# Loading the first eight heads of v by partition halves in an attention-times-value kernel

## The chip, the cores and the metric

The kernel runs on one core of a Trainium2 chip. A core has five engines with their own instruction streams: TensorE (PE) multiplies and transposes, VectorE (DVE) and ScalarE (ACT) copy between the memories, GpSimd (POOL) and SyncE (SP) issue the DMA transfers here, and POOL also builds masks and does one cast. Sixteen DMA engines move data between HBM and the on-chip memory SBUF, which has 128 partitions; matmuls write to PSUM. Time is the device time of one execution in microseconds (us); lower is better.

## The reference

```python
batch, n_heads, seq, head_dim = 8, 12, 1024, 64
attn_weights: (8, 12, 1024, 1024) fp32;  v: (8, 12, 1024, 64) fp32

return np.einsum('bhqs,bhsd->bhqd', attn_weights, v).astype(np.float32)
```

For each of 96 heads a 1024 x 1024 matrix is multiplied by a 1024 x 64 matrix. attn_weights is 403 MB, v and the output 25 MB each.

## The kernel before

Heads are taken four at a time (`VH = 4`): 24 groups q, each split into two units, 48 units n in all. Unit n is one load of attn_weights, `load_attn(n)`: 128 partitions x 16 row groups x 1024, cast from fp32 to bf16 by the DMA itself, 4096 KB in SBUF, into one of two buffers `abf[n % 2]`. All such loads are issued by POOL on its queue; in a loop over n, POOL waits until PE has transposed unit n, then issues the load of unit n + 2. Loads 0 and 1 are issued ahead of everything, and are called loads by their unit number below; load 2 is the third.

For each unit PE transposes 16 groups (`transpose_g`, line 146 in the profile), DVE and ACT copy them to `at` (line 276), PE multiplies them with v (`multiply`, line 191), the products are copied to `ot` (line 288), transposed back (line 176) and copied to the output tile `osb` (line 259). In every first unit of a group PE first spreads the group's v: `spread_v` (line 163) reads `vr`, in which v lies as bf16 with eight heads over 128 partitions, 16 partitions to a head, 4096 elements to a partition. The spread result is copied to `vbf` (line 252). Before it, PE waits for `s_vr` to count the groups whose v is there (line 210).

v arrives in `vr` by casting DMAs on POOL's queue (`load_v`, line 352), eight or sixteen heads at a time, except the first eight heads, groups 0 and 1. These come as fp32 into two output slots of `osb` that are not used yet (`v32`), 2 MB on SP's own queue, in two transfers of 1 MB: the first half of the columns of all 128 partitions (line 136), issued before the block in which all engines work, and the second half of the columns (line 413), issued by SP inside it. The block begins for every engine when the first transfer has landed; only POOL's loads 0 and 1 are issued without that wait. DVE sets constants to zero (lines 327 to 331), and casts the first half in two instructions of 1024 columns (line 334). POOL makes the masks `ident` and `spread` (lines 372 and 383), which PE needs before its first transpose, then waits for the second transfer and for DVE's casts (`s_v0`), casts the second half (line 393, 2048 columns), and raises `s_vr` by 2. Only then does its loop begin, with the load of unit 2.

After its transfer SP raises two counters: `s_free`, which lets ACT write output slots, and `s_half`, on which PE waits in the middle of each unit and which holds PE back while a burst of stores is under way.

Of the kernel before, what the change touches and what calls it, by code (L numbers as in the profile page):

```python
# [10 lines left out]
def kernel(  # L11
# [18 lines left out]
    nc = tc.nc  # L30
# [4 lines left out]
    B, H, Q, S = attn_weights.shape  # L35
    D = v.shape[-1]
    NH = B * H
    P = 128
# [4 lines left out]
    HP = P // 2  # L43
    KW = S // (2 * P)
    SB = S // P
    V8 = 2 * VH
    VB = S // (P // V8) // SB
# [10 lines left out]
    V_SLOT = 4  # L58
    V_AT_ONCE = 4
    V_LOADS = {2: 2, **{q: V_AT_ONCE for q in range(V_AT_ONCE, NV, V_AT_ONCE)}}  # L60

    V_REST = ((0, P),)
    HALVED = NU - 2
    TOGETHER = 8
    BURSTS = {8: ((0, 8),), 16: ((8, 2), (10, 6))}
# [3 lines left out]
    def slot(q):  # L69
        return q % NO  # L70
# [12 lines left out]
    def v_n(q, fours):  # L83
        return v_h[ds(q * VH, fours * VH)].rearrange(
            "(n eight) (p r) d -> (eight p) n (r d)", eight=V8, p=P // V8
        )
# [17 lines left out]
    vr = sb("vr", [P, V_AT_ONCE // 2, VB, SB * D], bf16)  # L104
    vbf = sb("vbf", [P, SB, VH, D], bf16)
    ot = sb("ot", [P, GH, P], fp32)
    osb = sb("osb", [P, NO, 2 * G, D], fp32)

    v32 = osb[:, ds(V_SLOT, 2)].rearrange("p n r d -> p n (r d)")
    v_first = v_n(0, 2)[:, 0].rearrange("p (half x) -> p half x", half=2)  # L110
    vr_first = vr[:, 0].rearrange("p (half b) x -> p half (b x)", half=2)
    bank = [nc.alloc_psum_tensor(f"bank{i}", [P, 512], fp32).ap() for i in range(8)]
    pt = [b.rearrange("p (k j) -> p k j", k=KW) for b in bank[:4]]
    po = bank[4:6]
# [5 lines left out]
    s_v0, s_v = sem("s_v0"), sem("s_v")  # L120
# [11 lines left out]
    s_const, s_vr = sem("s_const"), sem("s_vr")  # L132

    s_half, s_free = sem("s_half"), sem("s_free")

    nc.sync.dma_start(out=v32[:, 0], in_=v_first[:, 0])

    with tc.tile_critical(sync_engine=mybir.EngineType.Pool, no_gpsimd_drain=True):
        pe = nc.tensor
# [189 lines left out]

        for h in range(2):  # L330
            nc.vector.memset(ot[:, :, ds(h * HP, HP)], 0.0).then_inc(s_ot)
        for half in range(2):
            part = ds(half * (SB * D * VB // 4), SB * D * VB // 4)
            last = nc.vector.tensor_copy(out=vr_first[:, 0, part], in_=v32[:, 0, part])  # L334
        last.then_inc(s_v0)
        engine(True)
        engine(False)
        nc.scalar.wait_ge(s_held, 16 * (BY_SYNC - HELD_FROM) // 2)
# [2 lines left out]
        pool = nc.gpsimd  # L341

        def load_attn(n):
            pieces = [(0, G)] if n < HALVED else [(0, GH), (GH, GH)]
            for g0, gn in pieces:
                pool.dma_start(  # L346
                    out=abf[n % 2][:, ds(g0, gn)].rearrange("p g s -> p (g s)"),
                    in_=attn_q[n // 2][:, ds((n % 2 * G + g0) * S, gn * S)],
                ).then_inc(s_abf[n % 2] if g0 == 0 else s_second[n], 16)

        def load_v(q, fours):
            pool.dma_start(  # L352
                out=vr[:, ds(q % V_AT_ONCE // 2, fours // 2)].rearrange("p n b x -> p n (b x)"),
                in_=v_n(q, fours),
            ).then_inc(s_v, 16)

        def store(q, fours, eng, done):
            eng.wait_ge(s_out, 2 * (q + fours) + 1)
            at_slot = osb[:, ds(slot(q), fours)].rearrange("p n r d -> p n (r d)")
            eng.dma_start(  # L360
                out=out_n(q, fours), in_=at_slot,
                **({"single_packet": True} if eng is pool and fours == 2 else {}),
            ).then_inc(done, 16)

        def store_2(q):
# [7 lines left out]
            out=ident,  # L373
            in_=ident,
# [9 lines left out]
            out=spread,  # L384
            in_=spread,
# [3 lines left out]
            pattern=[[-P, V8], [-1, P + VB - 1]],  # L389
            channel_multiplier=VB,  # L390
        ).then_inc(s_const)
        pool.wait_ge(s_v0, 16 * len(V_REST) + 1)
        pool.tensor_copy(out=vr_first[:, 1], in_=v32[:, 1]).then_inc(s_vr, 2)  # L393
        for n in range(NU - 2):
            q, i = n // 2, n % 2
            if i == 0 and q + 1 in V_LOADS:
                pool.wait_ge(s_sp, 4 * (q + 1))
                load_v(q + 1, V_LOADS[q + 1])
            pool.wait_ge(s_t[True], (n + 1) * PER_DVE)
            load_attn(n + 2)  # L400
            if i == 0 and q % TOGETHER == 0 and 0 < q <= HELD_FROM:
                for q0, fours in BURSTS[q]:
                    store(q0, fours, pool, s_osb)
# [5 lines left out]

        for p0, pn in V_REST:
            nc.sync.dma_start(
                out=v32[ds(p0, pn), 1], in_=v_first[ds(p0, pn), 1]
            ).then_inc(s_v0, 16)
        nc.sync.sem_inc(s_free, NO // 2)
        nc.sync.sem_inc(s_half, WHOLE[0])
        for k in range(1, NV // 2):
# [9 lines left out]
        for n in range(HALVED, NU):  # L428
# [8 lines left out]
            out=out_q[NV - 1], in_=osb[:, slot(NV - 1)].rearrange("p r d -> p (r d)")  # L437
# [35 lines left out]
```

## Time and profile before

| | us |
|---|---|
| median of 3 runs | 1051.83 |
| lowest and highest | 1051.76, 1052.38 |
| the profiled execution | 1051.83 |
| its span on the core | 1050.0 |

| engine | busy, us | share of the span |
|---|---|---|
| PE | 795.4 | 76% |
| DVE | 388.7 | 37% |
| ACT | 410.6 | 39% |
| POOL | 39.1 | 4% |

The span runs from the first instruction to the last. The page's slices give for each fortieth of it the busy share of each engine and of the 16 DMA engines in tenths. The timeline gives an instruction's start and duration, and in brackets how long the engine had been idle before it and what ended that; `x64` means 64 of them merged. In the timeline "SPq" and "POOLq" are the issuing of transfers, not their landing. A stretch view gives the busy time of every engine between two times, then the granted clock, the share of the DMA engines' time that packets took, and GB/s; a packet counts in the stretch in which it begins, so short stretches can have a share above 1. GB/s are bytes written: a load of attn_weights reads two bytes for each one that it writes.

### The profile page before, as it was taken

Reading aid. Unit: us, or ns where it says so; the run is one execution under the profiler, and the core shown is the slowest. Engines: PE = TensorE matmul, PEld = TensorE weight load, DVE = VectorE, ACT = ScalarE, POOL = GpSimd, SP = SyncE. Lnnn points to the kernel's source line nnn. Section 1 sums busy time; section 2 is a strip of 40 time slices with the busy share of each in tenths; the row PEclk is TensorE's granted clock in tenths of the full one; section 3 lists DMA queues with packets and bytes.
Section 4 is the critical chain, followed back from the end, with each engine's and each line's share of the span. In section 5 each row is a group of like instructions: output and inputs, shape, how many; then the busy total and the mean of one; then the engine's idle time right before and its main releaser. Section 6 shows DMA issues by size and latency. Waiting matters only on the chain.

```text
span 1050.0 us, 17183 instructions
## 1 busy us (share of the span) xinstructions
PE 795.4 (76%) x7304; PEld 708.4 (67%) x7304; DVE 388.7 (37%) x583; ACT 410.6 (39%) x493; POOL 39.1 (4%) x68
## 2 busy tenths in 40 slices
PE   0878789489789492887949779859568975887995
PEld 0777678478678482777848678647547865776885
DVE  1443344235334251343424344324223432453443
ACT  0444344335335251343425344334224433444443
POOL 1000000000000000000000000000000000000000
PEclk9989889799898796889879989889878988899898
DMA  9999999999999999999999999999999999999999
GB/s 232 229 218 219 217 216 212 217 220 218 217 218 216 212 216 379 217 218 217 207 218 220 220 218 217 207 224 212 324 275 217 218 206 220 217 220 220 209 218 352
DMA packets 12198, 240.20 MB, mean 229 GB/s; under 512 B 1056, under 2 KB 1056, under 8 KB 1056
## 3 DMA queue, kind: packets, MB, share of 16 engines
q0 software_dynamic: 11344, 233.84, 99.1%
q1 hardware_dynamic: 848, 6.29, 1.5%
q8 instruction: 3, 0.05, 0.0%
q14 instruction: 3, 0.02, 0.0%
HBM read 427.82 MB, written 25.17 MB: 431 GB/s over the span
## 4 chain that ended last, share of the span: by engine, by line
DMA 71%; PE 26%; issue 1%; POOL 0%; ACT 0%; DVE 0%; ACTq 0%; SPq 0%; POOLq 0%
DMA abf<-in_attn_weights_dram 63%; PE bank L146 22%; DMA out_dram<-osb 8%; PE bank L163 3%; PE bank L191 1%; PE bank L176 1%; POOL vr L352 0%; ACT vbf L252 0%; ACT osb L259 0%; DVE osb L259 0%; ACT ot L288 0%; POOL abf L346 0%; ACTq L259 0%; SPq L424 0%; SPq L423 0%
## 5 line engine op out<-in xcount | busy, mean ns | idle before, releaser
L146 PE MATMUL bank<-ident,abf 128*128 128x128 f32 x3072 | 430.0, 307 | 215.3 <-DMA abf<-in_attn_weights_dram 188.2
L146 PEld LDWEIGHTS bank<-ident,abf 128*128 128x128 f32 x3072 | 420.4, 212 | 227.1 <-DMA abf<-in_attn_weights_dram 195.6
L276 DVE COPY at<-bank 128x1024 bf16<-128x1024 bf16 x480 | 319.7, 689 | 405.1 <-PE bank L146 400.6
L276 ACT COPY at<-bank 128x1024 bf16<-128x1024 bf16 x288 | 287.9, 1012 | 332.0 <-PE bank L146 332.0
L191 PE MATMUL bank<-at,vbf 128*64 128x256 bf16 x3072 | 225.7, 285 | 0.0
L191 PEld LDWEIGHTS bank<-at,vbf 128*64 128x64 bf16 x3072 | 203.7, 111 | 19.4 <-issue 6.3
L288 DVE COPY ot<-bank 128x512 f32<-128x512 f32 x48 | 33.2, 692 | 208.6 <-PE bank L191 208.6
L288 ACT COPY ot<-bank 128x512 f32<-128x512 f32 x48 | 28.1, 585 | 185.9 <-PE bank L191 185.9
L163 PE MATMUL bank<-vr,spread 32*128 32x512 bf16 x768 | 87.0, 375 | 0.6 <-issue 0.2
L176 PE MATMUL bank<-ident,ot 128*128 128x128 f32 x392 | 62.4, 312 | 29.4 <-ACT vbf L252 28.7
L176 PEld LDWEIGHTS bank<-ident,ot 128*128 128x128 f32 x392 | 51.3, 159 | 41.4 <-ACT vbf L252 40.5
L259 ACT COPY osb<-bank 128x512 f32 (+1 forms) x97 | 53.4, 588 | 31.2 <-PE bank L176 29.3
L163 PEld LDWEIGHTS bank<-vr,spread 32*128 32x128 bf16 x768 | 35.2, 93 | 44.0 <-issue 1.7
L346 POOL DMA_DIRECT2D abf<-in_attn_weights_dram x50 | 26.9, 538 | 788.7 <-PE bank L146 787.7
L252 ACT CAST vbf<-bank 128x512 bf16<-128x512 f32 x48 | 25.8, 589 | 74.4 <-PE bank L163 74.4
L252 DVE CAST vbf<-bank 128x512 bf16<-128x512 f32 x48 | 30.9, 686 | 29.1 <-PE bank L163 29.1
L276 ACT ACT_TABLE_LOAD x12 | 15.4, 1283 | 6.7 <-DMA osb<-in_v_dram 6.5
L352 POOL DMA_DIRECT2D vr<-in_v_dram x6 | 4.0, 674 | 136.3 <-PE bank L163 136.3
L360 POOL DMA_DIRECT2D out_dram<-osb x5 | 3.9, 786 | 12.0 <-ACT osb L259 12.0
L393 POOL CAST vr<-osb 128x2048 bf16<-128x2048 f32 x1 | 1.9, 1889 | 22.0 <-DMA osb<-in_v_dram 22.0
L327 DVE MEMSET ident<- 128x128 f32 x1 | 0.2, 165 | 6.5 <-DMA osb<-in_v_dram 6.5
L334 DVE CAST vr<-osb 128x1024 bf16<-128x1024 f32 x2 | 2.2, 1138 | 0.0
(9 smaller groups left out, 5.3 us busy)
## 6 DMA issues: line engine op xcount, KB each, us to landing
abf<-in_attn_weights_dram POOLq DMA_DIRECT2D x46, 4096.0 KB, 29.2
vr<-in_v_dram POOLq DMA_DIRECT2D x5, 2048.0 KB, 15.3
out_dram<-osb POOLq DMA_DIRECT2D x1, 8192.0 KB, 41.7
abf<-in_attn_weights_dram POOLq DMA_DIRECT2D x4, 2048.0 KB, 23.0
out_dram<-osb POOLq DMA_DIRECT2D x3, 2048.0 KB, 33.4
out_dram<-osb POOLq DMA_DIRECT2D x1, 6144.0 KB, 41.7
osb<-in_v_dram SPq DMA_DIRECT2D x2, 1024.0 KB, 15.7
out_dram<-osb SPq DMA_DIRECT2D x1, 2048.0 KB, 14.4
```

Of the source, the lines that this page charges most:

```text
L146: last = pe.matmul(out=pt[g % 4][:, k], lhsT=words[:, k], rhs=ident, is_transpose=True, start=(k == 0), stop=(k == KW - 1),)
L163: last = pe.matmul(out=banks[h], lhsT=spread[rows, j, ds(VB - 1 - b, P)], rhs=vr[rows, n // 2, b], start=(b == 0), stop=(b == VB - 1),)
L176: last = pe.matmul(out=ps[:, ds(j * P, P)], lhsT=ot[:, j0 + j], rhs=ident, is_transpose=True, start=(j == 0), stop=(j == jn - 1),)
L191: last = pe.matmul(out=outs, lhsT=vbf[:, 2 * kw + par, h], rhs=at[:, ds(half * GH, GH), kw, ds(h * VP, VP), par], start=(n == 0), stop=(n ...
L252: copy(out=vbf[:, :, h], in_=ps.rearrange("p (k d) -> p k d", k=SB)).then_inc(s_vbf)
L259: return copy(out=rows.rearrange("p (half j) d -> p j half d", half=2)[:, ds(j0, jn)], in_=ps[:, ds(0, jn * P)].rearrange("p (j half d) -> ...
L276: ins = copy(out=at[:, g].rearrange("c k j two -> c (k j two)"), in_=bank[g % 4].bitcast(bf16),)
L288: copy(out=ot.rearrange("c j (h p) -> c h j p", h=VH)[:, ds(2 * e, 2)], in_=po[e].rearrange("c (h j p) -> c h j p", h=2, j=GH),).then_inc( ...
L334: last = nc.vector.tensor_copy(out=vr_first[:, 0, part], in_=v32[:, 0, part])
L346: pool.dma_start(out=abf[n % 2][:, ds(g0, gn)].rearrange("p g s -> p (g s)"), in_=attn_q[n // 2][:, ds((n % 2 * G + g0) * S, gn * S)],).th ...
L352: pool.dma_start(out=vr[:, ds(q % V_AT_ONCE // 2, fours // 2)].rearrange("p n b x -> p n (b x)"), in_=v_n(q, fours),).then_inc(s_v, 16)
L360: eng.dma_start(out=out_n(q, fours), in_=at_slot, **({"single_packet": True} if eng is pool and fours == 2 else {}),).then_inc(done, 16)
```

## The change

The first eight heads of v still come as 2 MB of fp32 on SP's queue, but are cut by heads and not by columns: heads 0 to 3 lie on partitions 0 to 63, heads 4 to 7 on partitions 64 to 127.

- Ahead of the block SP issues two transfers of 512 KB: partitions 0 to 63, first and second half of the columns. Inside it, one transfer of 1 MB: partitions 64 to 127, all 4096 columns.
- DVE casts partitions 0 to 63 in two instructions of 2048 columns, and raises `s_vr` by 1 itself: group 0's v is there.
- POOL does not cast ahead of its loop. In the loop's first turn, after the load of unit 2, it waits for the third transfer, casts partitions 64 to 127 in one instruction of 4096 columns, and raises `s_vr` by 1 for group 1.

```diff
-    v32 = osb[:, ds(V_SLOT, 2)].rearrange("p n r d -> p n (r d)")
-    v_first = v_n(0, 2)[:, 0].rearrange("p (half x) -> p half x", half=2)
-    vr_first = vr[:, 0].rearrange("p (half b) x -> p half (b x)", half=2)
+    v32 = osb[:, ds(V_SLOT, 2)].rearrange("p n r d -> p (n r d)")
+    v_first = v_n(0, 2)[:, 0]
+    vr_first = vr[:, 0].rearrange("p b x -> p (b x)")
+    four = [ds(0, HP), ds(HP, HP)]
+    VC = S * V8 * D // P // 2
+    part = [ds(0, VC), ds(VC, VC)]
...
-    nc.sync.dma_start(out=v32[:, 0], in_=v_first[:, 0])
+    for x in part:
+        nc.sync.dma_start(out=v32[four[0], x], in_=v_first[four[0], x])
...
-        for half in range(2):
-            part = ds(half * (SB * D * VB // 4), SB * D * VB // 4)
-            last = nc.vector.tensor_copy(out=vr_first[:, 0, part], in_=v32[:, 0, part])
-        last.then_inc(s_v0)
+        for x in part:
+            last = nc.vector.tensor_copy(out=vr_first[four[0], x], in_=v32[four[0], x])
+        last.then_inc(s_vr)
...
-        pool.wait_ge(s_v0, 16 * len(V_REST) + 1)
-        pool.tensor_copy(out=vr_first[:, 1], in_=v32[:, 1]).then_inc(s_vr, 2)
         for n in range(NU - 2):
...
             load_attn(n + 2)
+            if n == 0:
+                pool.wait_ge(s_v0, 16)
+                pool.tensor_copy(out=vr_first[four[1]], in_=v32[four[1]]).then_inc(s_vr)
...
-        for p0, pn in V_REST:
-            nc.sync.dma_start(
-                out=v32[ds(p0, pn), 1], in_=v_first[ds(p0, pn), 1]
-            ).then_inc(s_v0, 16)
+        nc.sync.dma_start(out=v32[four[1]], in_=v_first[four[1]]).then_inc(s_v0, 16)
```

More of the change, by code (lines that the diff above doesn't have):

```diff
@@ L60 @@
     V_LOADS = {2: 2, **{q: V_AT_ONCE for q in range(V_AT_ONCE, NV, V_AT_ONCE)}}
-    V_REST = ((0, P),)
     HALVED = NU - 2
```

## The prediction

> **What bounds the kernel now.** I read the page's 40 slices and queue shares first, then the chain, then the start of the timeline, then busy time by stretch.
>
> ```profile
> span 1050.0 us, 17183 instructions
> ...
> DMA  9999999999999999999999999999999999999999
> ...
> q0 software_dynamic: 11344, 233.84, 99.1%
> q1 hardware_dynamic: 848, 6.29, 1.5%
> HBM read 427.82 MB, written 25.17 MB: 431 GB/s over the span
> ...
> DMA 71%; PE 26%; issue 1%; POOL 0%; ACT 0%; DVE 0%; ACTq 0%; SPq 0%; POOLq 0%
> ...
> abf<-in_attn_weights_dram POOLq DMA_DIRECT2D x46, 4096.0 KB, 29.2
> ...
> osb<-in_v_dram SPq DMA_DIRECT2D x2, 1024.0 KB, 15.7
> ```
>
> The 16 DMA engines are busy in every slice, and the two queues' packets fill 100.6% of them: POOL's queue q0 carries the loads of attn_weights, SP's q1 the first 2 MB of v and the last stores. The chain is 71% DMA; its 26% of PE is the wait of a load that may only be issued when its buffer has been read. Whether that wait empties the queues is read from the timeline's start:
>
> ```profile
> 27.68 9.31 PE L146 MATMUL bank<-ident,abf 128*128 128x128 f32 x64 [27.68 <-DMA abf<-in_attn_weights_dram]
> 37.23 3.63 PE L163 MATMUL bank<-vr,spread 32*128 32x512 bf16 x32 [0.24 <-issue]
> 37.30 0.57 POOL L346 DMA_DIRECT2D abf<-in_attn_weights_dram  x1 [3.00 <-PE bank L146]
> 39.20 1.29 DVE L252 CAST vbf<-bank 128x512 bf16<-128x512 f32 x2 [1.48 <-PE bank L163]
> 47.76 7.95 PE L146 MATMUL bank<-ident,abf 128*128 128x128 f32 x64 [0.21 <-DMA abf<-in_attn_weights_dram]
> 56.02 0.53 POOL L346 DMA_DIRECT2D abf<-in_attn_weights_dram  x1 [18.16 <-PE bank L146]
> 67.13 3.26 PE L146 MATMUL bank<-ident,abf 128*128 128x128 f32 x14 [6.13 <-DMA abf<-in_attn_weights_dram]
> ```
>
> Load 0 lands at 27.7 us, load 1 at about 47.5, load 2 at 67.1. Load 2 is issued at 37.30, ten microseconds before load 1 has drained, and load 3 at 56.02, eleven before load 2 has. So the queue never runs dry: engine time that PE, POOL or DVE lose here is hidden as long as it stays under about ten microseconds, and time that the DMA engines lose is not hidden by anything. The stretches say the same (columns: stretch, then each engine's busy time, granted clock, DMA share, GB/s written):
>
> ```profile
> 0.00:1.50 1.50, 0.00 (x0) 0.00 (x0) 0.00 (x0) 0.00 (x0) 0.36 (x5) 1.00 0.00 0
> 47.50:67.10 19.60, 13.29 (x137) 12.69 (x136) 7.33 (x11) 8.21 (x10) 0.53 (x1) 0.95 1.00 216
> 952.10:971.40 19.30, 13.23 (x137) 12.68 (x137) 7.33 (x11) 9.48 (x11) 0.53 (x1) 0.95 1.01 217
> ```
>
> Nothing moves before 1.5 us; a load then takes 67.13 - 47.76 = 19.4 us, near the start and near the end alike. Its 4096 KB are 128 rows of 32 KB, eight for each of 16 engines, 2.42 us each, writing 216 GB/s (the source is fp32, so it reads twice that).
>
> **The change part by part.** *The first transfers.* Before, 1 MB of v over 128 partitions goes first:
>
> ```profile
> 0.74 0.38 SPq L136 DMA_DIRECT2D osb<-in_v_dram  x1
> 1.34 1.23 POOL L346 DMA_DIRECT2D abf<-in_attn_weights_dram  x2 [0.90 <-POOLq L457]
> 6.33 0.33 SPq L413 DMA_DIRECT2D osb<-in_v_dram  x1
> 6.47 0.17 DVE L327 MEMSET ident<- 128x128 f32 x1 [6.47 <-DMA osb<-in_v_dram]
> ```
> ```profile
> 1.00:2.00 1.00, 0.00 (x0) 0.00 (x0) 0.00 (x0) 0.00 (x0) 0.66 (x1) 1.00 0.39 74
> 2.00:3.00 1.00, 0.00 (x0) 0.00 (x0) 0.00 (x0) 0.00 (x0) 0.57 (x2) 1.00 0.80 229
> 3.00:4.00 1.00, 0.00 (x0) 0.00 (x0) 0.00 (x0) 0.00 (x0) 0.00 (x0) 1.00 0.85 360
> 4.25:4.50 0.25, 0.00 (x0) 0.00 (x0) 0.00 (x0) 0.00 (x0) 0.00 (x0) 1.00 0.93 393
> 4.75:5.00 0.25, 0.00 (x0) 0.00 (x0) 0.00 (x0) 0.00 (x0) 0.00 (x0) 1.00 4.87 1147
> ```
>
> The packets count in the stretch in which they start, so the jump at 4.75 is the first large packets of load 0: from 1.5 to about 4.75 us the engines carry v alone, at up to 393/0.93 = 423 GB/s, which is 3.3 GB/s into each of 128 partitions. No row shows any partition taking more. After the change the same bytes go in two transfers to 64 partitions, so at the old rate each would have to take twice as much. That is the disputed price. Lower end: the writes follow, cost 0. Upper end: packets to half the partitions take twice as long. In the page's row q1 fills 1.5% of 16 x 1050 us = 252 us with 768 data packets of 8 KB (6.29 MB; the other 80, 16 for each of its five transfers, only count up semaphores), 0.33 us each; v's 2.1 MB are 256 of them, 84 us, or 5.25 us on each of the 16 engines. Doubled, that is +5.25 us.
>
> I place it between the ends by what writes beside it, with 212 GB/s (half of 423) as the ceiling for half the partitions. While v is alone: 2 to 3 us falls from 229 to 212, 3 to 4 from 360 to 212, the last 0.75 us from about 420 to 212, and the slow first microsecond stays: 17 + 148 + 156 = 321 KB late, which is 0.76 us at 423 GB/s. Those 321 KB, 2.5 packets per engine, then alternate with load 0's packets, and the third transfer (4096 elements on 64 partitions, four packets of 16 KB per engine, 0.66 us each by doubling 0.33) alternates throughout. There the extra is at most 2.5 x 0.33 + 4 x 0.66 = 3.5 us, if the engines that write to the same partitions always do so in step, and near 0 if they are out of step, since all others then write only load 0 at 216 GB/s over 128 partitions. The start is common to all engines, which speaks for in step; the long packets between drift. I take half, 1.75 us. Sum: 0.76 + 1.75 = +2.5 us.
>
> [...] No row here shows a transfer to 64 partitions.
>
> *The wait to begin.* All engines but POOL's first two loads wait for the first transfers: DVE's memset and ACT's table load start at 6.47, ended by that DMA. With 2.5 packets per engine left at 4.75, each behind a 2.42 us packet of load 0, the first transfers land about 2.5 x (2.42 + 0.66) = 7.7 us later, near 14. Behind that stand DVE's memsets, POOL's two masks, and SP's third transfer:
>
> ```profile
> 8.01 0.28 POOL L372 TENSOR_SCALAR_AFFINE_SELECT ident<-ident 128x128 f32<-128x128 f32 x1 [5.43 <-DVE spread L328]
> 8.43 1.97 POOL L383 TENSOR_SCALAR_AFFINE_SELECT spread<-spread 128x1080 bf16<-128x1080 bf16 x1
> 32.41 1.89 POOL L393 CAST vr<-osb 128x2048 bf16<-128x2048 f32 x1 [22.00 <-DMA osb<-in_v_dram]
> ```
>
> PE may start when the masks are done, 10.40 - 6.47 = 3.9 us after the entry: near 18 us, against load 0's 27.7. Cost 0; the entry would have to be after 23.7 to make PE late and after about 33 to empty the queue. SP's releases of half units and output slots stand behind its third transfer, first needed by PE in the middle of unit 0, after 30 us: hidden too.
>
> *DVE's casts.* Two of 64 x 2048 in place of two of 128 x 1024.
>
> ```profile
> L334 DVE CAST vr<-osb x2: 629/1138/1646, 8.8 to 9.3; 128x1024 bf16<-128x1024 f32 x2
> ```
>
> By columns they double: from 2 x 1.26 to 2 x 3.3 us (the 1646 ns one ran beside POOL's mask). They end by 14 + 2.5 + 6.6 = 23 us, and PE reads them at 37.23: 0. Their increment alone now releases PE's first spreading of v.
>
> *POOL's cast* moves behind load 2. It took 1.89 us for 2048 columns; for 4096, 1.9 us if it goes by elements and 3.8 by columns; I take 3.8, from 37.9 to 41.7. Being taken from ahead of load 2 gains nothing: it ended at 34.30, and the row of 37.30 shows load 2 waiting 3.00 us more, for PE. Queued behind it on POOL is load 3, at 56.02; the third transfer, issued near 14, lands by 14 + 4 x (2.42 + 1.31) = 29 plus a few microseconds, so its wait is over. Beside it run DVE's two casts of 39.20. Lower bound of the delay 0, upper 3.8 us if POOL keeps DVE out; unit 0 then ends near 51.5, unit 1's load 3 is issued near 60, still seven before load 2's landing at 67.1. Cost 0 at either end.
>
> *The sum* against the profiled execution: 1051.83 us, which is the median of the runs itself (span 1050.0 and 1.8 around it), + 2.5 = 1054.3 us.
>
> **The rivals.** *Full halving:* all 5.25 us, in step throughout, 1057.1. For it: a common start for all engines; against it: 88% of the traffic it alternates with writes at half the rate (2.42 of 2.75 us).
>
> *The halves cost nothing:* 1051.8. An engine that reads ahead could go on reading load 0 while v's writes drain: a load writes half of what it reads, so its write side has room. For it, 216 GB/s written in stretches where 423 have been seen. Against it, the first three microseconds have no load to read. If reading ahead hides all of the alternation, +0.8 remains, 1052.6, also no change by the bound.
>
> *Faster, a tighter start:* from 1.5 to about 47.5 us the engines need 46.0 us for two loads and v, where 2 x 19.4 + 5.25 = 44.0 would do. If two shorter transfers queued back to back and a third in half as many packets recover that, -2.0 us, 1049.8. Place: the DMA shares of 0.39 to 0.85 in the first three microseconds. It decides where the first transfers' packets take less than 1.2 times as long as before. Against it: the ramp is that of the first packets, whoever issues them.
>
> *The late entry binds:* slower, if the first transfers land after 33 us; 1 us for each beyond. The 2.5 packets late would have to be more than eight; next to excluded.
>
> **How the numbers follow.** Forecast (partial halving, own range 1053.3 to 1056.0) 0.47, of which 0.05 ends within 0.2% (2.1 us, below 1053.9; about what a measurement of this kernel can tell from no change); full halving 0.25; nothing or nearly nothing 0.20; tighter start 0.07, of which 0.05 beyond the bound, since its price could be short by what the trace does not show; late entry 0.01. Slower 0.42 + 0.25 + 0.01 = 0.68, same 0.05 + 0.20 + 0.02 = 0.27, faster 0.05. The range reaches from 1051.6, just under the free case, to 1057.2, just over the full one: what it leaves out is the tighter start and the tails.
>
> **What the changed profile would show.** Right: the first v transfers land near 14 us and not 6; q1's share rises from 1.5% to 1.7 or 1.8%; PE's units 1 and 2 start near 50 and 69.6 us where they started at 47.76 and 67.13, and the end is later by that same 2.5 us, with loads still 19.4 us apart. POOL's cast stands after load 2's issue with no wait for its DMA. Wrong: unit 2 starts at 67.1 or earlier (the halves are free, or the start tighter), or the shift of unit 2 is not the shift of the end, which would put the cause somewhere else than in these 2 MB.

## The result

| | us |
|---|---|
| before, median of 9 runs (lowest, highest) | 1051.84 (1051.73, 1052.38) |
| changed, median of 9 runs (lowest, highest) | 1054.59 (1054.03, 1057.14) |
| changed, the profiled execution | 1057.1, span 1055.3 |
| ratio changed to before | 1.0031, 95% interval 1.0022 to 1.0041 |

The changed kernel is slower by about 2.75 us. It also spreads over 3.1 us where the kernel before spreads over 0.65, and the execution that was profiled is one of the slowest, 5.3 us over the profiled one of before. The queue rows of its page, to hold against those of before:

```profile
DMA  9999999999999999999999999999999999999998
...
q0 software_dynamic: 11344, 233.84, 98.7%
q1 hardware_dynamic: 800, 6.29, 1.7%
q8 instruction: 3, 0.05, 0.0%
q14 instruction: 3, 0.02, 0.0%
HBM read 427.82 MB, written 25.17 MB: 429 GB/s over the span
```

The bytes are the same, the engines are as full, and SP's queue q1 takes 1.7% of their time where it took 1.5%. The start of the timeline shows where the end came from (the columns are start, duration, instruction, and the idle time before it):

```profile
0.74 1.18 SPq L139 DMA_DIRECT2D osb<-in_v_dram  x2
19.06 0.47 SPq L415 DMA_DIRECT2D osb<-in_v_dram  x1
19.22 0.17 DVE L330 MEMSET ident<- 128x128 f32 x1 [19.22 <-DMA osb<-in_v_dram]
21.52 3.25 DVE L336 CAST vr<-osb 64x2048 bf16<-64x2048 f32 x2
29.68 9.38 PE L149 MATMUL bank<-ident,abf 128*128 128x128 f32 x64 [29.68 <-DMA abf<-in_attn_weights_dram]
39.35 0.57 POOL L348 DMA_DIRECT2D abf<-in_attn_weights_dram  x1 [15.67 <-PE bank L149]
39.97 3.59 POOL L403 CAST vr<-osb 64x4096 bf16<-64x4096 f32 x1
51.95 7.95 PE L149 MATMUL bank<-ident,abf 128*128 128x128 f32 x64 [2.33 <-DMA abf<-in_attn_weights_dram]
71.27 1.13 PE L149 MATMUL bank<-ident,abf 128*128 128x128 f32 x4 [6.09 <-DMA abf<-in_attn_weights_dram]
```

The block begins at 19.2 us and not at 6.5; that costs nothing here, since PE still starts when load 0 lands (29.68). Units 0, 1 and 2 start 2.0, 4.2 and 4.1 us later than before (27.68, 47.76, 67.13). The loads after that come as far apart as before (unit 4 starts at 114.79 where it started at 110.68, again 4.1 later), so all but the last 1.1 us of the 5.3 is lost before load 2 has landed. Most of that rest comes in two steps, between units 16 and 18 (the shift goes from 4.2 to 4.8 us) and between units 32 and 34 (4.9 to 5.3), where the two bursts of stores are issued; why is not shown. By stretch, the first microseconds (share of DMA time and GB/s are the last two columns):

```profile
1.00:2.00 1.00, 0.00 (x0) 0.00 (x0) 0.00 (x0) 0.00 (x0) 0.66 (x1) 1.00 0.00 0
2.00:3.00 1.00, 0.00 (x0) 0.00 (x0) 0.00 (x0) 0.00 (x0) 0.58 (x2) 1.00 1.02 197
4.25:4.50 0.25, 0.00 (x0) 0.00 (x0) 0.00 (x0) 0.00 (x0) 0.00 (x0) 1.00 3.85 786
```

With the engines full (a share of 1.02), v alone moves at 197 GB/s; before, it reached 393 at a share of 0.93. By the packet records, load 0's first long packet begins at 4.20 us (4.75 before), and most of the first sixteen in the half microsecond after it (the jump of the third row).

The trace also records each packet on q1. Their durations, taken from those records of the profiled executions, are what most of the experiments turn on:

| kernel | v alone, before load 0's first packet | then, beside load 0 | third transfer |
|---|---|---|---|
| before | 8 KB: 0.31 us when steady, 118 of the first transfer's 128 begun | 8 KB: 0.31 | 8 KB: 0.32 |
| changed | 8 KB: 0.59 on average, 60 of the first two transfers' 128 begun | 8 KB: 0.34 | 16 KB: 1.11 (0.62 to 1.57) |

So half of the first megabyte was left when load 0 began; it then alternated with load 0's rows of 2.43 us (the last of it begins at 15.8 us) at 0.34 us each, little more than the old 0.31, and the third transfer's rows took 1.11 us on average where 0.64 is twice the short row.

### The profile page after: what moved, and what is told of

It reads as the page before. It is cut to its first block, busy times and chain, and to the rows that moved or that the text cites. A ratio compares the mean times of both kernels' runs of the same rounds, so it can differ in the third digit from the quotient of the medians.

```text
span 1055.3 us, 17183 instructions
## 1 busy us (share of the span) xinstructions
PE 796.4 (75%) x7304; PEld 708.7 (67%) x7304; DVE 389.7 (37%) x583; ACT 410.9 (39%) x493; POOL 41.4 (4%) x68
## 4 chain that ended last, share of the span: by engine, by line
DMA 71%; PE 26%; issue 1%; POOL 0%; ACT 0%; DVE 0%; ACTq 0%; SPq 0%; POOLq 0%
DMA abf<-in_attn_weights_dram 63%; PE bank L149 22%; DMA out_dram<-osb 8%; PE bank L166 3%; PE bank L194 1%; PE bank L179 1%; POOL vr L354 0%; ACT vbf L255 0%; ACT osb L262 0%; DVE osb L262 0%; ACT ot L291 0%; POOL abf L348 0%; ACTq L262 0%; SPq L424 0%; SPq L423 0%
## 5 line engine op out<-in xcount | busy, mean ns | idle before, releaser
L279 ACT ACT_TABLE_LOAD x12 | 15.4, 1283 | 19.4 <-DMA osb<-in_v_dram 19.2
L330 DVE MEMSET ident<- 128x128 f32 x1 | 0.2, 165 | 19.2 <-DMA osb<-in_v_dram 19.2
L403 POOL CAST vr<-osb 64x4096 bf16<-64x4096 f32 x1 | 3.6, 3591 | 0.0
L336 DVE CAST vr<-osb 64x2048 bf16<-64x2048 f32 x2 | 3.2, 1662 | 0.0
```

Source lines behind the costliest of these rows:

```text
L279: ins = copy(out=at[:, g].rearrange("c k j two -> c (k j two)"), in_=bank[g % 4].bitcast(bf16),)
L403: pool.tensor_copy(out=vr_first[four[1]], in_=v32[four[1]]).then_inc(s_vr)
```

## The experiments

Two theories at the start. *Halves:* writing to 64 of the 128 partitions is what costs. *Order:* the other edits cost it, that is two transfers in place of one ahead of the block, the late start of the block, or the moved cast.

**cols_order: all of the change but the halves** (the first two transfers are now quarters of the columns, the third the other half; the casts follow the same cut, and POOL raises `s_vr` by 2 for both groups; these edits are left out below)

```diff
-        nc.sync.dma_start(out=v32[four[0], x], in_=v_first[four[0], x])
+        nc.sync.dma_start(out=v32[:, x], in_=v_first[:, x])
...
-        nc.sync.dma_start(out=v32[four[1]], in_=v_first[four[1]]).then_inc(s_v0, 16)
+        nc.sync.dma_start(out=v32[:, rest], in_=v_first[:, rest]).then_inc(s_v0, 16)
```

> Everything of the changed kernel is kept (two transfers ahead of the block, POOL's cast behind load 2) but the cut: v is again cut by columns, every transfer to 128 partitions. Theory of the halves (writes to 64 partitions are slower): the loss is gone, 1051.5 to 1052.3, the first transfers land near 6.5 us, PE's unit 2 starts near 67.1. Rival (two transfers in place of one, or the moved cast, cost the time): 1054 to 1057 as the changed kernel.

Measured: 1053.31 us median (1052.38 to 1055.31), ratio 1.0015, interval 1.0006 to 1.0024. This is neither theory's number. Its timeline shows why it is no clean comparison:

```profile
38.29 1.90 POOL L404 CAST vr<-osb 128x2048 bf16<-128x2048 f32 x1
41.19 6.29 PE L167 MATMUL bank<-vr,spread 32*128 32x512 bf16 x32 [3.77 <-POOL vr L404]
63.95 0.53 POOL L349 DMA_DIRECT2D abf<-in_attn_weights_dram  x1 [23.76 <-PE bank L150]
```

Cut by columns, group 0 needs POOL's half too, which now comes behind load 2: PE waits 3.77 us, then runs the spreading in 6.3 us where it took 3.6 (the granted clock was 0.56 from 41.2 to 47.5 us; before, it was 1.00 from 37.2 to 40.9), and load 3 is issued at 63.95, eight microseconds later than before. A moved cast needs a cut by heads; front_split below is the control that this run was meant to be. What makes up the 1.4 us of this run stays open: in its profiled execution, 0.9 us over before, all 40 slices of the page have the DMA engines busy for 90% or more.

**front_halves: only the first transfer in halves** (the rest as before)

```diff
-    nc.sync.dma_start(out=v32[:, 0], in_=v_first[:, 0])
+    for p0 in (0, HP):
+        nc.sync.dma_start(out=v32[ds(p0, HP), 0], in_=v_first[ds(p0, HP), 0])
```

> The kernel before, with only the transfer ahead of the block cut into partitions 0 to 63 and 64 to 127 (512 KB each); the third transfer goes to 128 partitions. Theory of the halves: four of eight packets per engine are still to come when load 0's packets begin, 4 x 0.32 us = 1.3 us, so 1052.6 to 1053.6, and the block begins near 19 us and not 6.5; unit 2 starts near 68.4. Rival (the late block costs the time, not the packets): the whole loss, 1054 to 1057. Rival (only the 1 MB transfer with 16 KB rows costs): 1051.8.

Measured: 1060.08 us median (1059.54 to 1061.03), ratio 1.0081, interval 1.0067 to 1.0094: three times the loss of the whole change. The halves theory missed by 7 us, and the late block, which it had called hidden, is the reason:

```profile
19.14 0.35 SPq L414 DMA_DIRECT2D osb<-in_v_dram  x1
45.10 1.89 POOL L394 CAST vr<-osb 128x2048 bf16<-128x2048 f32 x1 [21.87 <-DMA osb<-in_v_dram]
46.94 0.57 POOL L347 DMA_DIRECT2D abf<-in_attn_weights_dram  x1
47.99 7.01 PE L164 MATMUL bank<-vr,spread 32*128 32x512 bf16 x32 [10.71 <-POOL vr L394]
71.60 0.53 POOL L347 DMA_DIRECT2D abf<-in_attn_weights_dram  x1 [24.09 <-PE bank L147]
```

and the stretches in which the queues ran dry:

```profile
46.00:48.00 2.00, 0.01 (x2) 0.02 (x3) 0.00 (x0) 0.00 (x0) 1.51 (x2) 0.50 0.01 0
68.00:70.00 2.00, 2.00 (x19) 2.00 (x18) 1.58 (x4) 1.57 (x3) 0.00 (x0) 1.00 0.01 0
70.00:72.00 2.00, 2.00 (x19) 1.93 (x18) 1.85 (x3) 1.52 (x3) 0.40 (x1) 1.00 0.04 8
```

The block begins at 19, the third transfer is issued only then, and it lands at 45: its eight rows per engine come one at a time between the rows of loads 0 and 1 (in the kernel before, such rows begin from 9.8 to 29.2 us, one every 2.8 us on each engine, the 2.43 of a load's row and 0.32); POOL casts, and only then issues load 2, at 46.94 in place of 37.30. In 46 to 48 us no large packet begins. The longer dry stretch is the second one. PE's spreading waits for the same cast, 10.71 us, and then takes 7.01 us where it took 3.63 (the granted clock was 0.50), so load 3 is issued at 71.60 in place of 56.02; load 2's last row ends at 69.6 us, and load 3's first begins at 72.8. Load 2's first row comes 2.3 us later than before, load 3's 7.6 us, and the end 7.7.

**third_halves: only the third transfer in halves, rows of 8 KB** (the rest as before)

```diff
-    V_REST = ((0, P),)
+    V_REST = ((0, HP), (HP, HP))
```

> The kernel before, with only the transfer inside the block cut into partitions 0 to 63 and 64 to 127 (two of 512 KB, packets of 8 KB). The block begins at 6.5 us as before. Theory of the halves: between 0 (packets out of step) and +2.6 us (each packet doubled while it alternates with load 0's), 1052 to 1054.4, most likely 1053. Rival (late block): 1051.8, no change.

Measured: 1052.03 us median (1051.83 to 1053.74) against 1051.94; ratio 1.0004, interval 0.9995 to 1.0013. This is no difference that can be told. The third transfer's packets took 0.33 us on average, where before, to all partitions, they took 0.32. So beside the loads here, rows of 8 KB to half the partitions are next to free; the doubling that I had allowed for is not there.

**pool_first: the changed kernel with POOL's cast ahead of load 2 again**

```diff
+        pool.wait_ge(s_const, 4)
+        pool.wait_ge(s_v0, 16)
+        pool.tensor_copy(out=vr_first[four[1]], in_=v32[four[1]]).then_inc(s_vr)
         for n in range(NU - 2):
...
-            if n == 0:
-                pool.wait_ge(s_v0, 16)
-                pool.tensor_copy(out=vr_first[four[1]], in_=v32[four[1]]).then_inc(s_vr)
```

> The changed kernel with POOL's cast back ahead of its loop, so ahead of load 2, waiting for the third transfer near 39 us; load 2 is then issued near 42 and not 39. Theory of the halves: still hidden, since load 1 drains near 51; 1054 to 1057 as the changed kernel. Rival (the place of the cast matters): at least 1 us away from the changed kernel's median of 1054.6.

Measured: 1054.32 us median (1053.82 to 1055.04), ratio 1.0022, interval 1.0013 to 1.0032, the same as the changed kernel. Its timeline:

```profile
37.27 3.60 POOL L396 CAST vr<-osb 64x4096 bf16<-64x4096 f32 x1 [13.38 <-DMA osb<-in_v_dram]
40.81 0.57 POOL L348 DMA_DIRECT2D abf<-in_attn_weights_dram  x1
50.94 7.95 PE L149 MATMUL bank<-ident,abf 128*128 128x128 f32 x64 [2.17 <-DMA abf<-in_attn_weights_dram]
69.72 2.62 PE L149 MATMUL bank<-ident,abf 128*128 128x128 f32 x11 [5.55 <-DMA abf<-in_attn_weights_dram]
```

Here four long rows per engine land by 37.3, and load 2 at 40.81 is still nine microseconds ahead of the end of load 1's last row, at 49.8. Unit 2 is 2.6 us late, and this execution (1054.4) ends 2.6 us late: the whole loss of such a run is there before load 2 lands.

**third_cols: the changed kernel with the third transfer in rows of 8 KB**

```diff
-                pool.wait_ge(s_v0, 16)
+                pool.wait_ge(s_v0, 32)
...
-        nc.sync.dma_start(out=v32[four[1]], in_=v_first[four[1]]).then_inc(s_v0, 16)
+        for x in part:
+            nc.sync.dma_start(out=v32[four[1], x], in_=v_first[four[1], x]).then_inc(s_v0, 16)
```

> The changed kernel with its third transfer (partitions 64 to 127, rows of 16 KB) cut in two by columns, so that each packet is 8 KB; the partitions are the same. In the cut of the kernel before (third_halves) packets of 8 KB to 64 partitions took 0.34 us beside load 0, hardly more than on 128 partitions; in the changed kernel those of 16 KB took 0.62 to 1.57. Theory that a long row cannot hide behind a load's packets where a short one can: the third transfer's share of the loss goes, 1052.6 to 1053.6, unit 2 starts near 68.4. Theory that 64 partitions cost the same whatever the row: 1054 to 1057, as the changed kernel.

Measured: 1053.78 us median (1052.96 to 1055.49), ratio 1.0017, interval 1.0008 to 1.0026, beside 1055.45 for the changed kernel on the same chip (after_again). This is just outside the range given, on the side of the row length: by these medians 1.7 us of the loss go with rows cut in two, on the same partitions (1.0 if the first set's loss of 2.75 is set against this run's 1.7). Its third transfer's packets took 0.36 us on average, where half of the changed kernel's 1.11 would be 0.55, and unit 2 starts at:

```profile
68.77 3.48 PE L149 MATMUL bank<-ident,abf 128*128 128x128 f32 x15 [6.16 <-DMA abf<-in_attn_weights_dram]
```

**front_split: only the first transfer in two, on all partitions** (the rest as before)

```diff
-    nc.sync.dma_start(out=v32[:, 0], in_=v_first[:, 0])
+    for x in (ds(0, S), ds(S, S)):
+        nc.sync.dma_start(out=v32[:, 0, x], in_=v_first[:, 0, x])
```

> The kernel before, with only its first transfer cut in two by columns (two of 512 KB to 128 partitions). If two issues in place of one cost something at the start: +0.3 to +0.5 us, 1052.2. If partitions are what counts: 1051.8 within 0.3, block begins near 6.5 us.

Measured: 1052.34 us median (1052.19 to 1052.72) against 1052.07; ratio 1.0003, interval 0.9994 to 1.0012. Not clear of zero, but its profile's unit 2 starts 0.5 us late (67.65), so two transfers in place of one may cost some 0.3 us.

**after_again: the changed kernel once more**

> The changed kernel once more, for its spread: 1054.0 to 1057.1 again. If the spread comes from how many engines write the 16 KB rows in step with each other, the profile's shift of unit 2 against 67.13 goes with the time: about 2.3 us in a run of 1054, 4.1 in one of 1057.

Measured: 1055.45 us median (1054.51 to 1056.95), ratio 1.0031, interval 1.0021 to 1.0042. The profiled execution (1056.7) has unit 2 at 71.35, 4.2 us late, with third-transfer rows of 1.10 us; pool_first's (1054.4) has 2.6 us and 0.98. The shift goes with the time, as far as three profiles tell. Why the loss of the slow ones exceeds the mean growth of the packets (four rows x 0.47 = 1.9 us, and about 1 for the first megabyte) is not shown, nor is the cause of the 1.1 and 0.7 us that the two profiled executions of the changed kernel lose later on.

**quarters and eighths: fewer partitions to a transfer** (four of 32, or eight of 16, rows of 16 KB; here the first edit for the 16, the third transfer is cut alike)

```diff
-    for x in part:
-        nc.sync.dma_start(out=v32[four[0], x], in_=v_first[four[0], x])
+    for p0 in range(0, HP, 16):
+        nc.sync.dma_start(out=v32[ds(p0, 16)], in_=v_first[ds(p0, 16)])
...
```

> The changed kernel with each transfer of v cut by partitions once more: four of 32 partitions by 4096 columns, rows of 16 KB. [...] If each partition has a ceiling of its own: packets near 2.6 us, at least 3 us more, above 1058.

> The changed kernel with v in eight transfers of 16 partitions by 4096 columns, one row of 16 KB per engine each. [...] If any cut below 128 partitions costs the same factor of two: 1055.7 as quarters.

Measured: quarters 1055.71 us (1055.17 to 1057.35), ratio 1.0036, interval 1.0022 to 1.0050; eighths 1063.97 us (1062.55 to 1064.98), ratio 1.0109, interval 1.0092 to 1.0126. 16 KB rows took 1.21 us while v was alone in quarters, which is what 64 partitions take for two of 8 KB (1.17), and 1.73 on average in eighths (up to 2.34 in some rows beside the loads). A ceiling for each partition would have made the rows of quarters four times the 0.59 of the changed kernel's 8 KB, about 2.4 us. The stretch from 2 to 3 us, in quarters:

```profile
2.00:3.00 1.00, 0.00 (x0) 0.00 (x0) 0.00 (x0) 0.00 (x0) 0.58 (x2) 1.00 1.16 262
```

and in eighths:

```profile
2.00:3.00 1.00, 0.00 (x0) 0.00 (x0) 0.00 (x0) 0.00 (x0) 0.58 (x2) 1.00 1.00 131
```

Per unit of DMA time that is 226 and 131 GB/s, beside 193 for 64 partitions in the same stretch; for 128 it is 286 there, while the first packets are still slow, and 423 from 4.25 to 4.50 us. By the median row, 8 KB took 0.31 us on 128 partitions and 0.60 on 64, and 16 KB took 1.28 on 32 and 1.88 on 16. So in these runs halving 128 partitions doubled the time for the same bytes (0.31 to 0.60), halving 64 did next to nothing (1.20 for two of 0.60, and 1.28), and halving 32 cost again (1.28 to 1.88). That is not a ceiling for each partition, which would have doubled the time at every step. What sets the rate instead, no run shows.

**third_cols_first: does the place of the cast matter when the third transfer is late?** (third_cols with the edit of pool_first)

> The changed kernel with the third transfer cut by columns (as third_cols, 1053.8) and POOL's cast back ahead of its loop. The third transfer then lands near 49 us, when load 1 has drained too; load 2 can only be issued after the cast, near 53. If front_halves lost its 8 us to this wait (queue dry until load 2's first packets), the loss comes back: load 1 drains near 49.4, load 2 issued near 53, and 3.4 us more to its first packet as at the start: about +7 us on third_cols, 1059 to 1062. If the place of the cast is of no matter, 1053.8.

Measured: 1060.45 us median (1059.69 to 1061.27), ratio 1.0082, interval 1.0065 to 1.0099: +6.7 us on third_cols, as a dry queue would have it.

```profile
48.52 3.60 POOL L396 CAST vr<-osb 64x4096 bf16<-64x4096 f32 x1 [24.79 <-DMA osb<-in_v_dram]
52.06 0.57 POOL L348 DMA_DIRECT2D abf<-in_attn_weights_dram  x1
75.27 9.85 PE L149 MATMUL bank<-ident,abf 128*128 128x128 f32 x64 [12.43 <-DMA abf<-in_attn_weights_dram]
```

```profile
48.00:50.00 2.00, 1.78 (x23) 1.48 (x20) 0.17 (x1) 0.58 (x1) 1.48 (x1) 1.00 0.00 0
50.00:52.00 2.00, 2.00 (x19) 2.00 (x19) 1.34 (x2) 1.14 (x3) 2.00 (x1) 1.00 0.00 0
```

The timeline has the third transfer landing at 48.5 and load 2 issued at 52.06; in the two stretches no packet that carries data begins. Load 1's last row ends at 49.3 us and load 2's first begins at 53.3, 1.3 us after its issue. Here group 0's v does not wait for POOL, and load 3 is issued at 57.85, in time; so this run shows what a late load 2 costs by itself, and front_halves was mostly a late load 3.

## Why the prediction was right, and where it was not

The forecast was 1054.3 us, slower with 0.68; measured were 1054.59 and, in a later set of runs, 1055.45. Its mechanism held in the main: what is lost is time of the DMA engines in writing half of the partitions (0.7 and 1.9 us more of each for the two megabytes of v, in the table below), and it reaches the end. It had named as a sign of being wrong a shift of unit 2 that is not the shift of the end. In pool_first and third_cols the two are the same (2.6 and 1.6 us); in the two profiled executions of the changed kernel they are 4.1 and 5.3, and 4.2 and 4.9, so about 1 us of these is lost later, by a cause that stays open.

That the median lies within 0.3 us of the forecast is in part luck: the half taken for the alternation was a choice that no row settled, and the runs of the changed kernel differ among themselves by 3.1 us. The packet records give the account of the start, in us for each of the 16 engines, from one profiled execution each:

| | before | third_cols | pool_first | changed |
|---|---|---|---|---|
| first packet of v begins | 1.80 | 2.07 | 2.09 | 2.08 |
| packets of v ahead of the block, 1 MB | 2.96 | 3.40 | 3.48 | 3.65 |
| packets of the third transfer (the second, before), 1 MB | 2.56 | 2.89 | 3.93 | 4.43 |
| rows of loads 0 and 1 | 38.94 | 39.27 | 39.23 | 39.44 |
| all four, more than before | | 1.4 | 2.5 | 3.3 |
| unit 2 starts later by | | 1.6 | 2.6 | 4.1 |

- *v alone, 0.76 us with 2.5 packets per engine left.* The size was near, its inside was not. Four of eight packets were left when load 0's began, but load 0's began 0.55 us earlier than before, so the first megabyte took 0.69 us more of each engine. Its first packet also came 0.28 us later, a cost that the working had not named. The ceiling of 212 GB/s was near (197 measured), but not for the reason given, 3.3 GB/s into each partition: in quarters 226 GB/s went into 32 partitions, 7 into each.
- *The alternation, half of 3.5 us.* Near in sum, wrong inside. The late packets of the first transfer cost 0.34 us each, not up to 0.66, and third_halves puts rows of 8 KB at 0.1 us in all, not clear of zero. The cost sits in the third transfer's 16 KB rows: 1.87 us more of each engine, 0.33 when they are cut in two (third_cols). The working had 1.3 for them, half of 4 x 0.66, and nothing for the rows of the loads, which took 0.5 us more. Whether engines are in step, on which I had made the choice, no run shows, nor whether an engine reads ahead in a load meanwhile, on which a rival rested; the length of the row is what the runs show.
- *The split by runs:* third_cols is 1.7 us over before, and after_again another 1.7 over third_cols. These two make after_again's 3.4 us (1055.45 - 1052.07) by subtraction alone, so the sum is no check. The table, from other records, is one: of the 4.1 us at unit 2 it has 3.3 for the mean engine, and load 1's last row ends 3.8 us later than before (51.2 against 47.4).
- *The wait to begin, cost 0.* Right for the changed kernel, with the entry at 19.2 in place of 14 (four packets to alternate, not 2.5). The bound of 33 us for the entry was reckoned for this kernel, whose cast stands behind load 2, and no run tries it there. It does not carry over to a kernel with the cast ahead of load 2: in front_halves an entry at 19 costs 8 us, because the third transfer is issued at the entry and POOL's cast, load 2 and PE's spreading wait for it. What keeps the changed kernel clear of that is the moved cast, or the short third transfer (pool_first).
- *POOL's cast moved, gain 0.* Right by pool_first; but as a cover it is worth 6.7 us where the third transfer lands late (third_cols_first).
- *The casts.* DVE 3.25 us for both (2.5 to 6.6 given), POOL 3.59 (3.8 taken), DVE's copies beside it 1.29 as before: hidden, as said.
- *Slack.* "Ten microseconds" counted to the end of load 1. Before, the first engine is done with load 1 and begins load 2 at 45.9 us, and with empty queues a load's first packet came 1.3 us after its issue (third_cols_first, front_halves), so the slack from 37.30 to an idle engine is nearer seven.

## What to carry to other kernels

Here the DMA engines are busy in every slice of the page, and the time that the transfers to 64 partitions took from them at the start (2.6 us more of each engine in the profiled execution) was paid at the end, even though everything that waits for these transfers was idle anyway. In a kernel of this kind, cut by columns over all 128 partitions when the consumer allows it (rows of 8 KB alone: 0.31 us, and 0.60 on 64), or keep the rows beside a load short: 8 KB rows to half of the partitions cost nothing that could be told (third_halves, 1052.03 us against 1051.94). Before moving a wait, follow the transfer that is issued behind it as well as the instructions: the 8 us of front_halves came from two loads that were only issued late, one behind POOL's cast and one behind PE's spreading.

## What the runs showed that I had not expected

Beside the loads of attn_weights, a row of 8 KB to half the partitions took 0.33 to 0.37 us on average and one of 16 KB 0.98 to 1.11, three times as long for twice the bytes; alone, the short one takes 0.60 (the median). Why, no run shows; the length of the row and the number of rows are not separated. Two transfers issued by SP in direct succession took 0.54 and 0.58 us each to issue on 64 partitions and 0.86 together on 128 (front_split). On 64 partitions the first packet also began later, at 2.08 us where it began at 1.80 before and at 1.78 in front_split.
